# A trunk layer on one core: earlier loads at the MLP's two borders and six residual buffers in a projection's tail

## The chip, the cores and the metric

The kernel runs on one core of a Trainium2 chip. The metric is the device time of one execution in microseconds. Before the change it is 3756.28 us, the median of three runs (3750.0 to 3760.29). Five engines work side by side, each in the order of its own instruction list: TensorE (PE) multiplies, VectorE (DVE), ScalarE (ACT) and GpSimd (POOL) work on tiles, and SyncE (SP) issues most of the DMA transfers. An instruction that waits holds all that stand behind it on its engine; SP's list is a queue of transfers in the same sense.

## The reference, cut to what matters

One layer over 2048 positions of width 1024, in float32:

```
for l in range(DEPTH):                       # DEPTH = 1
    proj = rms_norm(h, norm_mix_w[l]) @ w_in[l]
    y_rwkv = rwkv7_group(proj[..., :RWKV_COLS], ...)       # scan, width 512
    y_diff = diff_attn_group(proj[..., RWKV_COLS:], ...)   # block-causal, width 512
    h = h + concatenate([y_rwkv, y_diff], -1) @ w_out[l]
    h = h + memory_cross_attn(rms_norm(h, norm_mem_w[l]), rms_norm(mem, norm_src_w[l]), ...)
    hn = rms_norm(h, norm_mlp_w[l])
    h = h + square(relu(hn @ w_up[l])) @ w_down[l]         # 1024 -> 4096 -> 1024
return rms_norm(h, norm_final_w)
```

## The kernel before

Activations lie with features on the 128 partitions and 512 positions in a tile; a block is 512 positions, and there are four. Every large product is done in three passes: an operand is split into `hi` (an ACT copy to fp32r) and `lo = raw - hi` (DVE for activations, POOL for weights), and PE adds hi·hi, hi·lo and lo·hi. Weights come in halves of 128 x 4 x 128 (`wraw`, two buffers), and each half gives 12 matmuls of 128x512.

Three stages follow each other.

- **The first phase** runs the input projection as a list of `Item`s through `inproj_stream` (L599), which asks for weights two halves ahead (`li <= i + 2`), and between its pieces the RWKV units and attention. The list ends with 32 items from `wy_items` (L711), eight for each block: `w_out[0:512]` times the RWKV output, added to the residual. For each of them `pre(m)` loads a tile `xres` of the residual from the DRAM buffer `s_xT` (L731), `post(m)` adds the product to it on DVE (L738) and stores it back through ACT's queue (L739). `xres` takes its buffer from the tag `mix`, which has two. The last 24 of these items run in the tail of the phase with little else beside them.
- **The middle stage** (`m_stream` for blocks 0 and 1) isn't touched.
- **The last `m_stream`** takes blocks 2 and 3 together (`NSB == 2`, `s` = 0 and 1). Its MLP has two borders. `mo_forms` (L1296) ends the memory attention and builds for each k of 0 to 3 the seven operand forms that the fast scheme for the up projection needs ("11", "t1", "21", "22", "t3", "t2", "t4"), each split into `bfh` and `bfl`. `up_pairs` (L1341) then makes the hidden tiles two at a time, f = 0, 2, ..., 30 and a drain at 32, seven products of 12 matmuls for each pair, into `ps_a`, `ps_b` and `ps_c`; `emit` (L1363) stores each hidden tile to the DRAM buffer `s_hid`. After it, the down projection loads residual tiles `ht` and hidden tiles in four groups `fg` of eight: `load_hid` (L1533) loads `hraw`, ACT makes `hdh` (L1541), DVE makes `hdl` (L1542), and `down_mm` multiplies them with `w_down` (`load_w`, L161) into `ps_dn` (L186 to L188).

The program is written in one order, and a scheduler, which simulates a timeline while the program is built, sets the order on each engine from it.

Of the kernel before, what the change touches and what calls it, by code (L numbers as in the profile page):

```python
# [8 lines left out]
F32 = mybir.dt.float32  # L9
F32R = mybir.dt.float32r  # L10
# [6 lines left out]
P = 128  # L17
# [20 lines left out]
def f32(ap):  # L38
    return ap.bitcast(F32)
# [539 lines left out]
class Item:  # L579
    def __init__(self, blk, src, post, pre=None, n=TB, nh=2, vt=None):  # L580
        self.blk, self.src, self.post, self.pre, self.n, self.nh, self.vt = blk, src, post, pre, n, nh, vt


def fold_half(g, it, hf, w, st):
# [14 lines left out]
def inproj_stream(g, pool, items, st):  # L599
    nc = g.nc  # L600
    flat = [(it, hf) for it in items for hf in range(it.nh)]
    ready = []
    li = 0
    for i, (it, hf) in enumerate(flat):
        while li < len(flat) and li <= i + 2:
            it2, h2 = flat[li]
            raw = pool.tile([P, 4, P], F32, tag="wraw", name="wraw", bufs=2)
            if it2.vt:
                src = it2.src[h2 * P:(h2 + 1) * P].rearrange("p (k c) -> p k c", c=P)
            else:  # L610
                src = it2.src[h2 * 512:(h2 + 1) * 512].rearrange("(k p) c -> p k c", p=P)
            nc.sync.dma_start(out=raw, in_=src)
            hi = pool.tile([P, 4, P], F32R, tag="whi", name="whi", bufs=3)
            lo = pool.tile([P, 4, P], F32R, tag="wlo", name="wlo", bufs=3)
            nc.scalar.activation(out=hi, in_=raw, func=AF.Copy)  # L615
            nc.gpsimd.tensor_tensor(out=lo, in0=raw, in1=f32(hi), op=ALU.subtract)  # L616
            ready.append((hi, lo))
            li += 1
        if it.vt:
            yield from fold_half(g, it, hf, ready[i], st)  # L620
            continue
        if hf == 0:
            if it.pre:
                it.pre()
            ps = g.ps_acc.tile([P, TB], F32, tag="acc", name="ps_acc")
        hi, lo = ready[i]
        xs = st[it.blk][0]
        o = ps[:, 0:it.n]
        for kk in range(4):
            k = 4 * hf + kk  # L630
            nc.tensor.matmul(o, hi[:, kk, :], xs[k][0], start=(k == 0), stop=False)  # L631
            nc.tensor.matmul(o, hi[:, kk, :], xs[k][1], start=False, stop=False)  # L632
            last = k == 4 * it.nh - 1
            nc.tensor.matmul(o, lo[:, kk, :], xs[k][0], start=False, stop=last)  # L634
            if last:
                it.post(ps)
            yield
# [73 lines left out]
def wy_items(g, pool, st, blk, key):  # L711
    nc = g.nc
    cs = slice(blk * TB, (blk + 1) * TB)
    xts = {}

    def pre(m):
        def f():
            if m == 0:
                ys = []
                for k in range(4):  # L720
                    kk = k + 4 * ((blk + 1) % 2)
                    raw = pool.tile([P, TB], F32, tag="xsl", name="yraw", bufs=3)
                    nc.sync.dma_start(out=raw, in_=g.s.yT[k * P:(k + 1) * P, cs])
                    hi = pool.tile([P, TB], F32R, tag=f"xhi{kk}", name="yhi", bufs=1)
                    lo = pool.tile([P, TB], F32R, tag=f"xlo{kk}", name="ylo", bufs=1)
                    nc.scalar.activation(out=hi, in_=raw, func=AF.Copy)
                    nc.vector.tensor_tensor(out=lo, in0=raw, in1=f32(hi), op=ALU.subtract)
                    ys.append((hi, lo))
                st[key] = [ys]
            xt = pool.tile([P, TB], F32, tag="mix", name="xres", bufs=2)  # L730
            nc.sync.dma_start(out=xt, in_=g.s.xT[m * P:(m + 1) * P, cs])  # L731
            xts[m] = xt
        return f

    def post(m):
        def f(ps):
            xt = xts[m]
            nc.vector.tensor_tensor(out=xt, in0=ps, in1=xt, op=ALU.add)  # L738
            nc.scalar.dma_start(out=g.s.xT[m * P:(m + 1) * P, cs], in_=xt)  # L739
        return f  # L740
    return [Item(key, g.i.w_out[0, :, m * P:(m + 1) * P], post(m), pre(m), TB, 1) for m in range(KD)]


def phase1(g, er):
# [551 lines left out]
def mo_forms(g, mc, wp, fx, O, B, tsl, accs, tag):  # L1296
# [14 lines left out]
    for k in range(4):  # L1311
        bw = {}
        for e in range(2):
            m = k + 4 * e
            wh, wl = load_w(g, wp, g.s.mb[:, m * P:(m + 1) * P])
            for s in range(2):
                xt = mc.px.tile([P, TB], F32, tag="xt", name="xt", bufs=mc.nxt)
                nc.sync.dma_start(out=xt, in_=g.s.hT[m * P:(m + 1) * P, tsl[s]])
                ps = mc.ps_acc.tile([P, TB], F32, tag="acc", name="ps_mo2")
                yield from mm3g(g, ps, wh, wl, lambda k: O[k][s][0], lambda k: O[k][s][1])  # L1320
                nc.vector.tensor_tensor(out=xt, in0=ps, in1=xt, op=ALU.add)
                nc.scalar.dma_start(out=g.s.hT[m * P:(m + 1) * P, tsl[s]], in_=xt)
                b = fx.tile([P, TB], F32, tag="bw", name="bw", bufs=4)
                nc.scalar.activation(out=b, in_=xt, func=AF.Copy, scale=g.col("nmlp", m))
                add_stat(g, mc.px, xt, accs[s], m == 0, "h")
                bw[e, s] = b
                if e == 0 and s == 1:
                    nc.vector.tensor_tensor(out=bw[0, 0], in0=b, in1=bw[0, 0], op=ALU.subtract)
                    split("t1", bw[0, 0])
                else:  # L1330
                    split(("11", "21", "22")[e + s], b)
            yield
        nc.vector.tensor_tensor(out=bw[0, 1], in0=bw[1, 1], in1=bw[0, 1], op=ALU.subtract)
        split("t3", bw[0, 1])
        nc.vector.tensor_tensor(out=bw[0, 0], in0=bw[1, 1], in1=bw[0, 0], op=ALU.subtract)
        split("t2", bw[0, 0])
        nc.vector.tensor_tensor(out=bw[1, 0], in0=bw[1, 0], in1=bw[0, 0], op=ALU.subtract)
        split("t4", bw[1, 0])


def up_pairs(g, mc, wp, B, SB, mlp_scale, tag):  # L1341
# [30 lines left out]
    acc = lambda nm: mc.ps_acc.tile([P, TB], F32, tag="acc", name=nm)  # L1372
    tmp = lambda tg, nb, nm: wp.tile([P, TB], F32, tag=tg, name=nm, bufs=nb)
    prev = None
    for f in range(0, 33, 2):
        if f < 32:
            raw = {}
# [30 lines left out]
        if f < 32:  # L1408
            prod(a, split(raw[0, 1]), "21", False)
            emit(a, f, 0)  # L1410
            c = acc("ps_c")
            prod(c, split(s1), "t1", True)
            s3 = sub(raw[0, 0], raw[1, 0])
            prod(b, split(s3), "t3", False)
            r67 = tmp("wraw", 2, "r67")
            add(r67, b, p1)
            add(r67, c, r67)
            emit(r67, f + 1, 1)
            prev = (f, b, c, p1, r6, raw[1, 1], sub(raw[0, 1], s2))
            yield  # L1420


def m_stream(g, mc, wp, blk0, NSB, Y=None, ahead=None):
# [92 lines left out]
    if NSB == 2:  # L1516
        with ExitStack() as e2:
# [1 line left out]
            accs = [mc.px.tile([P, TB], F32, tag=f"acc{s}", name="acc", bufs=1) for s in range(NSB)]  # L1519
            B = {}  # L1520
            yield from mo_forms(g, mc, wp, fx, O, B, tsl, accs, t1)
            yield from up_pairs(g, mc, wp, B, SB, mlp_scale, t0)
    with ExitStack() as e2:
        ip = e2.enter_context(tc.tile_pool(name="p3b", bufs=2, reuse_waits="tile"))
        ht = [[None] * NSB for _ in range(KD)]
        for m in range(KD):
            for s in range(NSB):
                t = ip.tile([P, TB], F32, tag="ht", name="ht", bufs=mc.nact)
                nc.sync.dma_start(out=t, in_=g.s.hT[m * P:(m + 1) * P, tsl[s]])
                ht[m][s] = t  # L1530
        tg = (t0, t1)

        def load_hid(fg, f, rows):  # L1533
            r0 = (fg * KD + f) * P
            row = []
            for s in range(NSB):
                raw = ip.tile([P, TB], F32, tag="t", name="hraw", bufs=8)
                nc.sync.dma_start(out=raw, in_=g.s.hid[r0:r0 + P, s * TB:(s + 1) * TB])
                hi = act[s].tile([P, TB], F32R, tag=tg[fg % 2] + "h", name="hdh", bufs=KD)
                lo = act[s].tile([P, TB], F32R, tag=tg[fg % 2] + "l", name="hdl", bufs=KD)  # L1540
                nc.scalar.activation(out=hi, in_=raw, func=AF.Copy)  # L1541
                nc.vector.tensor_tensor(out=lo, in0=raw, in1=f32(hi), op=ALU.subtract)  # L1542
                row.append((hi, lo))
            rows.append(row)
        nxt = []
        if NSB == 2:
            for f in range(KD):
                load_hid(0, f, nxt)
        for fg in range(4):
            HID, nxt = nxt, []  # L1550
            for f in range(0 if NSB == 2 else KD):
                c0 = (fg * KD + f) * P
                wh, wl = load_w(g, wp, g.i.w_up[0, :, c0:c0 + P])
# [21 lines left out]
                nc.vector.tensor_tensor(out=ht[m][s], in0=ht[m][s], in1=ps, op=ALU.add)  # L1575
            if fg < 3:
                for m in range(KD):
                    w = down(m)
                    for s in range(NSB):
                        yield from down_mm(m, s, w)  # L1580
                    if NSB == 2:
                        load_hid(fg + 1, m, nxt)
                    yield
        for s in range(NSB):
            acc = mc.px.tile([P, TB], F32, tag=f"acc{s}", name="accf", bufs=1)
# [125 lines left out]
```

## Time and profile before

| what | value |
|---|---|
| median of three runs | 3756.28 us |
| profiled execution: its own time | 3755.66 us |
| its span, first to last instruction | 3753.9 us |
| mean granted TensorE clock | 0.966 |
| tail of the first phase (24 `xres` items) | 1307 to 1416 us |
| `mo_forms` to `up_pairs` | 3044 to 3057 us |
| `up_pairs` to the down projection | 3357 to 3384 us |

The views are read so. A row of waits says engine, waiting tile and line, then what it waited for, with the total in us, how many times, and the longest. A row of windows gives a stretch in us, its length, the busy time and count of PE, PE's weight loads, DVE, ACT and POOL, then the granted clock (1.00 is 2.4 GHz, 0.50 is 1.2 GHz), the busy share of the DMA engines and GB/s. A row of a timeline gives the start in us, the duration, engine, line, operation, output <- inputs and count, and in brackets how long the engine had been idle and what ended that; a row with a count above 1 joins several instructions, and its duration is their sum or stretch. For a DMA the duration is that of the issue, not of the transfer. A row of a tile gives line, engine and operation, count, the shortest, median and longest duration in ns, and the first and last start.

### The profile page before, as it was taken

How to read it: one execution, taken by the hardware profiler on the slowest of the kernel's cores; microseconds unless marked ns; L12 is line 12 of the kernel's file. 1: busy time of each engine (PE TensorE's matmuls, PEld its weight loads, DVE VectorE, ACT ScalarE, POOL GpSimd, SP SyncE). 2: the span in 40 equal slices, each digit the busy share in tenths (PEclk: the TensorE clock that was granted, in tenths of full speed). 3: DMA queues.
4: the chain of work that ended last, by engine and by line, in shares of the span. 5: the costliest groups of instructions: out<-in, count | busy, mean ns of one | idle time of the engine just before them, and what ended most of it. 6: DMA issues, size and time to landing. Idle time of an engine off the chain costs nothing. (4 is left out here: it accounts for less than half of the span.)

```text
span 3753.9 us, 58334 instructions
## 1 busy us (share of the span) xinstructions
PE 3549.6 (95%) x21105; PEld 2837.0 (76%) x21105; DVE 2075.2 (55%) x4201; ACT 1801.4 (48%) x3958; POOL 1538.8 (41%) x1243
## 2 busy tenths in 40 slices
PE   7999999999999878899999989999999999979998
PEld 5767767776767767678787777888878878868887
DVE  4456666675573636465566766666633565634212
ACT  5354464454455526554455765555543443323213
POOL 4524324423424534354535435353353364432235
PEclk9989999999989899999999999999999999989999
DMA  4343343333335674343323424232252243335223
GB/s 151 107 127 88 80 130 87 88 109 88 88 88 155 208 210 142 102 127 93 114 79 118 139 74 145 79 113 78 85 156 90 88 132 107 106 128 168 87 58 107
DMA packets 584503, 424.10 MB, mean 113 GB/s; under 512 B 67235, under 2 KB 493302, under 8 KB 584214
## 3 DMA queue, kind: packets, MB, share of 16 engines
q1 hardware_dynamic: 543350, 346.33, 31.7%
q10 hardware_dynamic: 37280, 67.13, 5.1%
q0 software_dynamic: 3584, 6.92, 0.8%
q8 instruction: 166, 2.72, 0.3%
q14 instruction: 123, 1.01, 0.1%
HBM read 327.92 MB, written 92.34 MB: 112 GB/s over the span
## 5 line engine op out<-in xcount | busy, mean ns | idle before, releaser
L170 POOL TENSOR_TENSOR wlo<-wraw,whi 128x512 fp32r<-128x512 f32 x456 | 609.1, 1337 | 1026.0 <-ACT whi L169 959.7
L616 POOL TENSOR_TENSOR wlo<-wraw,whi 128x512 fp32r<-128x512 f32 x288 | 414.2, 1440 | 591.6 <-ACT whi L615 489.3
L169 ACT ACTIVATE whi<-wraw 128x512 fp32r<-128x512 f32 x456 | 286.1, 628 | 494.5 <-PE ps_dn L187 300.0
L186 PE MATMUL ps_dn<-hdh,whi 128*128 128x512 f32 x1024 | 402.5, 395 | 21.4 <-ACT hdh L1541 19.6
L187 PE MATMUL ps_dn<-hdl,whi 128*128 128x512 f32 x1024 | 402.6, 394 | 0.3 <-DVE hdl L1566 0.3
L188 PE MATMUL ps_dn<-hdh,wlo 128*128 128x512 f32 x1024 | 400.0, 394 | 2.7 <-POOL wlo L170 2.7
L631 PE MATMUL ps_acc<-xhi,whi 128*128 128x512 f32 x832 | 341.4, 411 | 19.5 <-ACT carry L278 18.8
L634 PE MATMUL ps_acc<-xhi,wlo 128*128 128x512 f32 x832 | 342.5, 412 | 2.3 <-POOL wlo L616 2.3
L632 PE MATMUL ps_acc<-xlo,whi 128*128 128x512 f32 x832 | 339.7, 409 | 0.0
L615 ACT ACTIVATE whi<-wraw 128x512 fp32r<-128x512 f32 x288 | 180.4, 628 | 264.2 <-PE ps_acc L632 99.0
L1048 ACT ACTIVATE pt<-ps_s,nmx 128x512 f32<-128x512 f32 (+3 forms) x320 | 197.9, 619 | 143.9 <-DVE nmx L1047 118.8
L1575 DVE TENSOR_TENSOR ht<-ht,ps_dn 128x512 f32<-128x512 f32 x128 | 87.6, 684 | 306.6 <-PE ps_dn L188 306.3
L186 PEld LDWEIGHTS ps_dn<-hdh,whi 128*128 128x128 f32 x1024 | 193.8, 189 | 62.1 <-ACT hdh L1541 20.5
L1047 DVE TENSOR_REDUCE nmx<-ps_s 128x1 f32<-128x512 f32 (+3 forms) x320 | 192.3, 605 | 74.8 <-PE ps_s L1044 70.7
L188 PEld LDWEIGHTS ps_dn<-hdh,wlo 128*128 128x128 f32 x1024 | 193.5, 189 | 44.7 <-POOL wlo L170 5.7
L187 PEld LDWEIGHTS ps_dn<-hdl,whi 128*128 128x128 f32 x1024 | 193.6, 189 | 39.9 <-DVE hdl L1566 0.5
L631 PEld LDWEIGHTS ps_acc<-xhi,whi 128*128 128x128 f32 x832 | 160.4, 193 | 69.1 <-ACT carry L278 24.7
L186 PE MATMUL ps_up<-h2h,whi 128*128 128x512 f32 x512 | 201.2, 394 | 0.9 <-DVE t L1561 0.9
L188 PE MATMUL ps_up<-h2h,wlo 128*128 128x512 f32 x512 | 201.0, 393 | 0.8 <-POOL wlo L170 0.8
L187 PE MATMUL ps_up<-h2l,whi 128*128 128x512 f32 x512 | 201.4, 393 | 0.0
L634 PEld LDWEIGHTS ps_acc<-xhi,wlo 128*128 128x128 f32 x832 | 160.0, 192 | 49.9 <-issue 10.7
L632 PEld LDWEIGHTS ps_acc<-xlo,whi 128*128 128x128 f32 x832 | 160.1, 192 | 39.7 <-issue 7.0
(379 smaller groups left out, 8773.8 us busy)
## 6 DMA issues: line engine op xcount, KB each, us to landing
wraw<-in_w_in_dram SPq DMA_DIRECT2D x208, 256.0 KB
wraw<-in_w_down_dram SPq DMA_DIRECT2D x208, 256.0 KB
wraw<-in_w_up_dram SPq DMA_DIRECT2D x128, 256.0 KB
s_hT<-xt ACTq DMA_DIRECT2D x64, 256.0 KB
wfr<-in_w_up_dram SPq DMA_DIRECT2D x64, 256.0 KB
s_hid<-hid ACTq DMA_DIRECT2D x64, 256.0 KB
hraw<-s_hid SPq DMA_DIRECT2D x64, 256.0 KB
wraw<-in_w_out_dram SPq DMA_DIRECT2D x56, 256.0 KB
```

What stands on the lines that cost most here:

```text
L169: nc.scalar.activation(out=hi, in_=raw, func=AF.Copy)
L170: nc.gpsimd.tensor_tensor(out=lo, in0=raw, in1=f32(hi), op=ALU.subtract)
L186: nc.tensor.matmul(ps, whi(k), ahi(k), start=(k == 0), stop=False)
L187: nc.tensor.matmul(ps, whi(k), alo(k), start=False, stop=False)
L188: nc.tensor.matmul(ps, wlo(k), ahi(k), start=False, stop=(k == nk - 1))
L615: nc.scalar.activation(out=hi, in_=raw, func=AF.Copy)
L616: nc.gpsimd.tensor_tensor(out=lo, in0=raw, in1=f32(hi), op=ALU.subtract)
L631: nc.tensor.matmul(o, hi[:, kk, :], xs[k][0], start=(k == 0), stop=False)
L632: nc.tensor.matmul(o, hi[:, kk, :], xs[k][1], start=False, stop=False)
L634: nc.tensor.matmul(o, lo[:, kk, :], xs[k][0], start=False, stop=last)
L1047: nc.vector.tensor_reduce(out=nmx[:, m, c:c + 1], in_=ps[:, 0:w], axis=AX.X, op=ALU.max, negate=True)
L1048: nc.scalar.activation(out=pt[:, cw(c)], in_=ps[:, 0:w], func=AF.Exp, bias=nmx[:, m, c:c + 1], accum_out=sm[:, m, c:c + 1])
```

## The change

It has four parts. `xres` gets a tag of its own with six buffers, and its load moves out of `pre` into `load(m)`, which `inproj_stream` calls right after the item's weight transfer. In `mo_forms`, after each k, form t2 is built first, then t3 and t4, and the split of "22" goes last. `load_hid` becomes a function of its own that loads straight into the `lo` tile (`hdl`), from which ACT makes `hdh` and DVE subtracts in place, so that `hraw` and its eight buffers go; `up_pairs` itself loads the first group of hidden tiles, those of s = 0 inside the last pair (f = 30) and those of s = 1 after the drain. In the down projection the 16 `ht` loads go from ahead of everything to the place where each is first used in group 0, and group 0 begins with the weights of m = 0 and 1 together, both products of s = 0, then both of s = 1.

```
 inproj_stream:
             nc.sync.dma_start(out=raw, in_=src)
+            if it2.load:
+                it2.load()
 wy_items:
-            xt = pool.tile([P, TB], F32, tag="mix", name="xres", bufs=2)
+        return f
+
+    def load(m):
+        def f():
+            xt = pool.tile([P, TB], F32, tag="xres", name="xres", bufs=6)
             nc.sync.dma_start(out=xt, in_=g.s.xT[m * P:(m + 1) * P, cs])
             xts[m] = xt
 mo_forms:
-                else:
-                    split(("11", "21", "22")[e + s], b)
+                elif e + s < 2:
+                    split(("11", "21")[e], b)
             yield
+        nc.vector.tensor_tensor(out=bw[0, 0], in0=bw[1, 1], in1=bw[0, 0], op=ALU.subtract)
+        split("t2", bw[0, 0])
         nc.vector.tensor_tensor(out=bw[0, 1], in0=bw[1, 1], in1=bw[0, 1], op=ALU.subtract)
         split("t3", bw[0, 1])
-        nc.vector.tensor_tensor(out=bw[0, 0], in0=bw[1, 1], in1=bw[0, 0], op=ALU.subtract)
-        split("t2", bw[0, 0])
         nc.vector.tensor_tensor(out=bw[1, 0], in0=bw[1, 0], in1=bw[0, 0], op=ALU.subtract)
         split("t4", bw[1, 0])
+        split("22", bw[1, 1])
+def load_hid(g, mc, tag, f, s):
+    lo = mc.act[s].tile([P, TB], F32R, tag=tag + "l", name="hdl", bufs=KD)
+    hi = mc.act[s].tile([P, TB], F32R, tag=tag + "h", name="hdh", bufs=KD)
+    g.nc.sync.dma_start(out=f32(lo), in_=g.s.hid[f * P:(f + 1) * P, s * TB:(s + 1) * TB])
+    g.nc.scalar.activation(out=hi, in_=f32(lo), func=AF.Copy)
+    g.nc.vector.tensor_tensor(out=lo, in0=f32(lo), in1=f32(hi), op=ALU.subtract)
+    return hi, lo
 up_pairs:
+        if f == 30:
+            first.append([load_hid(g, mc, tag, i, 0) for i in range(KD)])
+    first.append([load_hid(g, mc, tag, i, 1) for i in range(KD)])
+    return first
 m_stream, down projection:
             if fg < 3:
                 for m in range(KD):
-                    w = down(m)
-                    for s in range(NSB):
-                        yield from down_mm(m, s, w)
+                    if NSB == 2 and fg == 0 and m != 1:
+                        for i in range(m, max(2, m + 1)):
+                            load_h(i)
+                    if NSB == 2 and fg == 0 and m < 2:
+                        ws = [down(0), down(1)] if m == 0 else ws
+                        for i in range(2):
+                            yield from down_mm(i, m, ws[i])
+                    else:
+                        w = down(m)
+                        for s in range(NSB):
+                            yield from down_mm(m, s, w)
                     if NSB == 2:
-                        load_hid(fg + 1, m, nxt)
+                        nxt.append([load_hid(g, mc, (t0, t1)[(fg + 1) % 2], (fg + 1) * KD + m, s) for s in range(2)])
```

SP's list at the border from `up_pairs` to the down projection, before: four `w_down` halves (`wraw`), 16 `ht`, eight `hraw`, then the next half. These rows are the last two `ht` and the rows up to that half.

```order
L1529 DMA ht_34026<-s_hT_61 128x512
L1529 DMA ht_34028<-s_hT_61 128x512
L1538 DMA hraw_34030<-s_hid_62 128x512
L1538 DMA hraw_34036<-s_hid_62 128x512
L1538 DMA hraw_34042<-s_hid_62 128x512
L1538 DMA hraw_34048<-s_hid_62 128x512
L1538 DMA hraw_34054<-s_hid_62 128x512
L1538 DMA hraw_34060<-s_hid_62 128x512
L1538 DMA hraw_34066<-s_hid_62 128x512
L1538 DMA hraw_34072<-s_hid_62 128x512
L166 DMA wraw_34278<-in_w_down_dram 128x4x128
```

The same place now. The first row stands behind 25 other loads of hidden tiles, which follow the last weights of the up projection; they belong to groups 0 and 1.

```order
L1355 DMA hdl_34059<-s_hid_62 128x512
L166 DMA wraw_34086<-in_w_down_dram 128x4x128
L1355 DMA hdl_34614<-s_hid_62 128x512
L1355 DMA hdl_34619<-s_hid_62 128x512
L166 DMA wraw_34092<-in_w_down_dram 128x4x128
L1355 DMA hdl_34064<-s_hid_62 128x512
L1355 DMA hdl_34692<-s_hid_62 128x512
L1355 DMA hdl_34697<-s_hid_62 128x512
L166 DMA wraw_34098<-in_w_down_dram 128x4x128
L1355 DMA hdl_34069<-s_hid_62 128x512
L1555 DMA ht_34078<-s_hT_61 128x512
```

What moved: the hidden tiles of two groups stand ahead of the first `w_down` half, and `ht` behind them all.

DVE's list at the end of `mo_forms` for one k, before: 31145 is the tile of t3, 31107 of t2, 31196 of t4 and 31234 of "22".

```order
L1333 TENSOR_TENSOR bw_31145<-bw_31234,bw_31145 128x512
L1335 TENSOR_TENSOR bw_31107<-bw_31234,bw_31107 128x512
L1309 TENSOR_TENSOR bfl_31240<-bw_31234,bfh_31239 128x512
L1337 TENSOR_TENSOR bw_31196<-bw_31196,bw_31107 128x512
L1309 TENSOR_TENSOR bfl_31245<-bw_31145,bfh_31244 128x512
L1309 TENSOR_TENSOR bfl_31250<-bw_31107,bfh_31249 128x512
L1309 TENSOR_TENSOR bfl_31255<-bw_31196,bfh_31254 128x512
```

And now:

```order
L1343 TENSOR_TENSOR bw_31107<-bw_31234,bw_31107 128x512
L1345 TENSOR_TENSOR bw_31145<-bw_31234,bw_31145 128x512
L1347 TENSOR_TENSOR bw_31196<-bw_31196,bw_31107 128x512
L1319 TENSOR_TENSOR bfl_31241<-bw_31107,bfh_31240 128x512
L1319 TENSOR_TENSOR bfl_31246<-bw_31145,bfh_31245 128x512
L1319 TENSOR_TENSOR bfl_31251<-bw_31196,bfh_31250 128x512
L1319 TENSOR_TENSOR bfl_31255<-bw_31234,bfh_31254 128x512
```

The t2 subtraction and its `bfl` come one and two places earlier, and the `bfl` of "22" is last.

SP's list near the start of the program, where the transposed input is stored to `s_xT` (`xsl`) and the first weights are loaded, before:

```order
L250 DMA s_xT_57<-xsl_274 128x512
L250 DMA s_xT_57<-xsl_288 128x512
L250 DMA s_xT_57<-xsl_302 128x512
L612 DMA wraw_233<-in_w_in_dram 128x4x128
L250 DMA s_xT_57<-xsl_316 128x512
L612 DMA wraw_371<-in_w_in_dram 128x4x128
L250 DMA s_xT_57<-xsl_330 128x512
```

And now:

```order
L250 DMA s_xT_57<-xsl_274 128x512
L738 DMA xres_11748<-s_xT_57 128x512
L738 DMA xres_11977<-s_xT_57 128x512
L250 DMA s_xT_57<-xsl_288 128x512
L738 DMA xres_12178<-s_xT_57 128x512
L250 DMA s_xT_57<-xsl_302 128x512
L250 DMA s_xT_57<-xsl_316 128x512
L613 DMA wraw_233<-in_w_in_dram 128x4x128
L613 DMA wraw_371<-in_w_in_dram 128x4x128
L738 DMA xres_12408<-s_xT_57 128x512
L250 DMA s_xT_57<-xsl_330 128x512
```

The first six residual loads, whose buffers nothing has used yet, have moved to the start of the program, each behind the store that it reads; the first `xres` load of the program before stood some 400 places later.

## Rows read from the trace of the kernel before

**Rows 1.** The page: busy time, share and count of each engine.
```profile
PE 3549.6 (95%) x21105; PEld 2837.0 (76%) x21105; DVE 2075.2 (55%) x4201; ACT 1801.4 (48%) x3958; POOL 1538.8 (41%) x1243
```

**Rows 2.** Waits of PE over the whole span: xres and the two borders.
```profile
PE ps_acc L631 <- DVE xres L738: 21.9, 12, 5.1
PE ps_dn L186 <- ACT hdh L1541: 19.6, 1, 19.6
...
PE ps_b L1360 <- ACT bfh L1308: 4.9, 1, 4.9
```

**Rows 3.** Timeline around the border from the up to the down projection.
```profile
3351.60 0.50 PE L1360 MATMUL ps_b<-bfh,wfh 128*128 128x512 f32 x1 [0.78 <-DVE r L1370]
...
3353.03 5.67 SPq L166 DMA_DIRECT2D wraw<-in_w_down_dram  x3
...
3356.32 0.63 ACT L169 ACTIVATE whi<-wraw 128x512 fp32r<-128x512 f32 x1 [2.66 <-DMA wraw<-in_w_down_dram]
...
3358.75 10.69 SPq L1529 DMA_DIRECT2D ht<-s_hT  x16
...
3369.75 6.31 SPq L1538 DMA_DIRECT2D hraw<-s_hid  x8
3376.40 5.25 ACT L1541 ACTIVATE hdh<-hraw 128x512 fp32r<-128x512 f32 x8 [16.77 <-DMA hraw<-s_hid]
...
3377.08 2.38 PE L186 MATMUL ps_dn<-hdh,whi 128*128 128x512 f32 x4 [19.63 <-ACT hdh L1541]
3377.12 5.25 DVE L1542 TENSOR_TENSOR hdl<-hraw,hdh 128x512 fp32r<-128x512 f32 x8 [18.15 <-ACT hdh L1541]
```

**Rows 4.** Windows: in mo_forms' border, the first down matmuls, the end of up_pairs.
```profile
3046.00:3048.00 2.00, 0.00 (x0) 0.00 (x0) 2.00 (x2) 0.63 (x1) 2.00 (x3) 0.50 0.41 122
...
3376.00:3380.00 4.00, 2.92 (x6) 2.10 (x7) 2.86 (x5) 3.35 (x6) 0.00 (x0) 0.50 1.06 389
3380.00:3384.00 4.00, 4.00 (x12) 3.08 (x12) 3.27 (x6) 3.06 (x6) 0.00 (x0) 0.57 1.03 356
...
3307.00:3357.00 50.00, 49.22 (x213) 39.57 (x212) 17.02 (x24) 15.11 (x26) 15.96 (x12) 1.00 0.21 72
```

**Rows 5.** Timeline around the border from mo_forms to up_pairs.
```profile
3046.81 1.75 DVE L1335 TENSOR_TENSOR bw<-bw 128x512 f32<-128x512 f32 x1
...
3049.27 0.80 PE L1360 MATMUL ps_b<-bfh,wfh 128*128 128x512 f32 x1 [4.92 <-ACT bfh L1308]
...
3056.76 0.65 PE L158 MATMUL psb<-ident,rstdg 128*128 128x128 f32 x4 [0.94 <-POOL rstdg L153]
```

**Rows 6.** Windows: the tail of the first phase.
```profile
1307.00:1416.00 109.00, 83.17 (x358) 65.34 (x357) 35.91 (x81) 27.68 (x59) 37.29 (x31) 0.93 0.71 207
```

**Rows 7.** Waits of PE, DVE and the SP queue in 1307 to 1416 us.
```profile
PE ps_acc L631 <- DVE xres L738: 20.8, 11, 5.1
PE ps_s L1043 <- DVE xres L738: 5.0, 1, 5.0
...
DVE xres L738 <- DMA xres<-s_xT: 62.4, 19, 7.9
...
SPq L731 <- DMA s_xT<-xres: 54.1, 19, 6.8
```

**Rows 8.** The tile xres in 1307 to 1416 us: its additions.
```profile
L738 DVE TENSOR_TENSOR xres<-ps_acc,xres x24: 683/692/693, 1316.3 to 1414.6; 128x512 f32<-128x512 f32 x24
```

**Rows 9.** Timeline in the tail: one turn of a weight buffer.
```profile
1354.43 0.40 SPq L612 DMA_DIRECT2D wraw<-in_w_out_dram  x1
...
1358.85 0.63 ACT L615 ACTIVATE whi<-wraw 128x512 fp32r<-128x512 f32 x1 [4.27 <-DVE xres L738]
...
1359.56 1.29 POOL L616 TENSOR_TENSOR wlo<-wraw,whi 128x512 fp32r<-128x512 f32 x1 [3.62 <-ACT whi L615]
...
1361.41 0.40 SPq L612 DMA_DIRECT2D wraw<-in_w_out_dram  x1
```

**Rows 10.** Timeline at the start of the program.
```profile
24.30 0.60 ACT L249 ACTIVATE xsl<-ps_xt 128x512 f32<-128x512 f32 x1 [0.47 <-DMA s_xT<-xsl]
```

More of the change, by code (lines that the diff above doesn't have):

```diff
@@ L581, in __init__ @@
         self.blk, self.src, self.post, self.pre, self.n, self.nh, self.vt = blk, src, post, pre, n, nh, vt
+        self.load = None
 def fold_half(g, it, hf, w, st):
@@ L740, in post @@
         return f
-    return [Item(key, g.i.w_out[0, :, m * P:(m + 1) * P], post(m), pre(m), TB, 1) for m in range(KD)]
+    out = [Item(key, g.i.w_out[0, :, m * P:(m + 1) * P], post(m), pre(m), TB, 1) for m in range(KD)]
+    for m, it in enumerate(out):
+        it.load = load(m)
+    return out
 def phase1(g, er):
@@ L1374, in up_pairs @@
     prev = None
+    first = []
     for f in range(0, 33, 2):
@@ L1521, in m_stream @@
             yield from mo_forms(g, mc, wp, fx, O, B, tsl, accs, t1)
-            yield from up_pairs(g, mc, wp, B, SB, mlp_scale, t0)
+            first = yield from up_pairs(g, mc, wp, B, SB, mlp_scale, t0)
     with ExitStack() as e2:
@@ L1525, in m_stream, with load_h @@
         ht = [[None] * NSB for _ in range(KD)]
-        for m in range(KD):
+        def load_h(m):
             for s in range(NSB):
@@ L1530, in m_stream @@
                 ht[m][s] = t
[L1531 to L1535, printed above, removed]
-            for s in range(NSB):
[L1537 to L1545, printed above, removed]
+        if NSB == 1:
+            for m in range(KD):
+                load_h(m)
         if NSB == 2:
-            for f in range(KD):
-                load_hid(0, f, nxt)
+            nxt = [list(r) for r in zip(*first)]
         for fg in range(4):
-            HID, nxt = nxt, []
+            HID, nxt = (nxt, []) if NSB == 2 else ([], [])
             for f in range(0 if NSB == 2 else KD):
@@ L1577, in m_stream @@
                 for m in range(KD):
-                    w = down(m)
-                    for s in range(NSB):
-                        yield from down_mm(m, s, w)
+                    if NSB == 2 and fg == 0 and m != 1:
[9 more added lines that the diff above has]
+                            yield from down_mm(m, s, w)
                     if NSB == 2:
-                        load_hid(fg + 1, m, nxt)
+                        nxt.append([load_hid(g, mc, (t0, t1)[(fg + 1) % 2], (fg + 1) * KD + m, s) for s in range(2)])
                     yield
```

## The prediction

> **What bounds the kernel now.** I read the page's busy times first: PE is busy 95% of the span and the next engine, PE's weight loads apart, 55% [rows 1]. So time can only come from where PE stands still or runs at the low clock. The waits of PE over the span name three such places that the change touches: 21.9 us for `xres` in the first phase, 19.6 us in one piece before the first down matmul, which waits for ACT's `hdh`, and 4.9 us at the entry of `up_pairs` [rows 2]. The timeline shows what stands behind the 19.6. The weights are early: SP begins to ask for `w_down` at 3353.03, and ACT copies the first half at 3356.32. But then SP issues 16 `ht` (10.69 us) and only at 3369.75 the `hraw` loads, whose first lands 6.65 us later, at 3376.40 [rows 3]. Nothing needs `ht` that early: a product is added to it only when it is done. The wait for `xres` lies nearly all in the tail of the first phase. In its 109 us PE is busy 83.17, idle 25.8, at a mean clock of 0.93 [rows 6]. In the waits 25.8 us of PE (20.8 and 5.0) stand against DVE's `xres`, DVE's `xres` stands 62.4 us against its DMA, and SP holds that load for 54.1 us until an earlier store of `xres` has landed [rows 7]. So the chain there is a ring: load, add, store, and the same buffer's next load. Its additions run from 1316.3 to 1414.6, 24 of them, 4.27 us apart in the mean [rows 8]; with two buffers one turn is twice that, 8.5 us.
>
> **The border from the up to the down projection.** Gone: the 19.63 us [rows 3], and the low clock after it. In 3377.08 to 3384.00, 6.9 us, 18 matmuls start [rows 4], where the step in the last 50 us of `up_pairs` is 49.22 / 213 = 0.231 us [rows 4], 4.2 us for 18. I put 2.5 us on it, since the last may reach over the edge. Together 22.1 us.
>
> Added: nothing in instructions (32 hidden tiles of groups 0 and 1 still need a load, an ACT copy and a DVE subtraction), but their place moves into the last 50 us or so of `up_pairs`, and 26 of the loads now stand ahead of the first `w_down` half on SP. Each waits until its buffer, a weight or form tile of the last pairs, is done with. The one just ahead of the first half takes a tile of the t3 product, which in the last pair has the products t4 and 22 behind it: 24 matmuls, 5.5 us before the end. The weights are thus asked for about 5.2 us before PE runs dry. A `w_down` half took at most 3.29 us from the request to ACT's copy, and a load in the burst 6.65 [rows 3]. With the first: landed at -1.9, the ACT copy (0.63) by about -0.9 since it queues behind a few `hdh`, the gap 0 to 1.5 us, as the third pass waits for POOL's `wlo`, 1.3 us more. With the second: landed at +1.5, PE dry for 2 to 3 us. I take 1 us, nearer the first row, since the DMA engines are at 0.21 there before [rows 4] and the hidden tiles come paced by their buffers.
>
> The cover for the moved work: DVE is busy 17.02 and ACT 15.11 of those 50 us [rows 4]. An `hdl` costs 5.25 / 8 = 0.66 us [rows 3], 32 of them 21 us, so DVE goes to about 38 of 50, and some are left for after the border. The new wait is on DVE: behind three `hdl` in its list stands the sum `r` of the last pair, for which PE already waited 0.78 us at 3351.60 [rows 3]. I expect this to become 1 to 2 us, so it costs 0.5. Net for this border: 22.1 - 1 - 0.5 = 20.6, ends 22 (all hidden) and 17 (PE dry for 3 us, `r` 2 us late).
>
> DVE's t2 subtraction took 1.75 us [rows 5] in a stretch in which POOL was busy without a break [rows 4], while `hdl`, with POOL idle [rows 4], took 0.66. The Trainium skill, "SBUF — State Buffer", section "Who interferes with whom", says that a DVE instruction with two SBUF inputs and a GpSimd instruction that reads SBUF shut each other out, since they share a port pair. The trace agrees, 1.75 against 0.66. If `hdl` tiles meet POOL's 12 instructions of the last 50 us [rows 4], each meeting costs DVE some 1.1 us, 13 us in all, and DVE would stand at 51 of 50 us: `r` and the tiles behind it would be some 4 us late. By the rule the border would gain 16 to 17 and the kernel take 3717; by the rows without it, 3713. I stay with the second, since the loads are paced by PE's products and need not meet POOL each time.
>
> **The border into `up_pairs`.** PE waits 4.92 us until ACT's `bfh` of t2 [rows 5]. That subtraction moves one place up, ahead of one of 1.75 us, so PE resumes some 1.7 us earlier. But it resumes into three or four matmuls and soon needs the `bfl` tiles and later the row scale `psb` (at 3056.76, 0.94 us of wait for POOL [rows 5]), which stands behind the same DVE work as before. What is won at the wait is lost there. I put 0, ends -1 (a loss) and 2.
>
> **The tail of the first phase.** With six buffers a turn of 8.5 us and even 12 us gives at most 2 us for an item, so the ring stops binding. Next are three bounds. PE: 83.17 us x 0.93 / 24 = 3.2 us an item at full clock [rows 6]. DMA: weights, load and store are 3 x 262 KB; the stretch moved 207 GB/s at a share of 0.71 [rows 6], so 292 GB/s full, 2.7 us. Weights: two `wraw` buffers, one turn from issue to issue 1361.41 - 1354.43 = 6.98 us [rows 9], or 3.5 an item; in it ACT's copy waited for DVE's `xres`, because the store's issue stands ahead of it on ACT, and without that it is shorter, say 3.3 to 3.8 with fuller DMA engines. I take 3.5. The most that can be won is the idle 25.8 and the clock's 83.17 x 0.07 = 5.8, 31.6 us. Of it the weights keep 24 x (3.5 - 3.2) = 7 and the entry and exit of the stretch (the 5.0 us wait [rows 7] is at its end) about 3: 22 us, ends 8 (3.9 us an item and a clock that stays low) and 31.
>
> **The rest.** Six `xres` loads come to the start of the program, each behind the landing of a store to `s_xT`. ACT's `xsl` already waits for such a landing at 24.30, 0.47 us [rows 10], so it costs a wait of SP of under a microsecond at each; weights stand behind it, but PE has work. I put 0.5 lost, ends 0 and 2. PE's waits for `xres` outside the tail are 21.9 - 20.8 = 1.1 us [rows 2, 7]: gain 1. Elsewhere the scheduler shuffles neighbours in phase one; I give that 0, ends -5 and 5.
>
> Sum: 20.6 + 22 + 0 - 0.5 + 1 = 43 us. The profiled execution took 3755.66, its median of three runs 3756.28, so 0.6 more; from there 3756.3 - 43 = 3713.
>
> **The rivals.**
> - *The weights bind the tail.* Fuller DMA engines stretch the landing until a turn of `wraw` is 7.8 us, 3.9 an item. For it: two buffers only, and a turn of 6.98 already. Against it: ACT's copy no longer waits for the store. Gain in the tail 8 instead of 22: 3727.
> - *The hidden tiles hold back the weights at the border.* 26 loads ahead of `w_down`, landings as in the burst (6.65 us), copies behind `hdh` on ACT: PE dry for about 6 us, and the low clock again for 2.5, with later halves late by about 1.5. The gain is 12: 3722. For it: SP's order. Against it: DMA at 0.21 there.
> - *The change doesn't do what it says.* `xres` isn't with the weights but where the scheduler puts it, as the six at the start show, so the ring of the tail only shifts (gain 4 or less), and the border gives 5 or less because the loads wait for buffers of the last pair: about 3748. Against it: from item 8 on, loads and weights alternate on SP.
> - *The tail becomes slower than before.* If loads, weights and stores come bunched, a weight lands late; `xres` once stood 7.9 us for its transfer [rows 7]. A `wraw` turn is landing plus 0.63 and 1.29 and a request, 2.3 us; the tail breaks even at a turn of 8.5, a landing of 6.2, and loses the border's 20.6 too at 24 x (period - 4.27) = 20.6, a period of 5.1, a landing of 8. At 9 us of landing: 5.65 an item, 33 lost, 12 net: 3768. One `xres` came near that; the mean did not.
>
> **How the numbers follow.** The forecast, both places gained: 0.65, its own range 3700 to 3724. Weights bind the tail 0.15, border held back 0.10, not as said 0.05, slower tail 0.05. A measurement of this kernel can tell some 0.3%, 11 us, from no change. The first three cases are all faster than that: 0.90; not as said is 0.05 for within it; slower 0.05. Both gains at their ends, 22 and 31, give 3702, with the shuffle's 5 us 3698; the two middle rivals reach 3727, together with a bad shuffle 3733. I take 3699 to 3733.
>
> **What would show it.** Right: no wait of PE over 3 us before the first down matmul and a granted clock of 1.00 through it, `hdl` and `hdh` inside the last pairs of `up_pairs`, PE's waits for `xres` in the tail under 5 us, and additions about 3.5 us apart. If they are 3.9 and PE waits for `whi` or `wlo` at L615 and L616, the weights bind. If the first down matmul waits for `whi`, the border is held back. If `r` or `hid` of the last pair waits long on DVE, the moved subtractions weren't covered. The prediction is wrong if either gain is under half of its term.

## The result, and the profile after

The changed kernel takes 3719.53 us (median of four runs, 3718.53 to 3731.22) against 3757.12 of the kernel before on the same chip (3750.0 to 3760.29, four runs): a ratio of 0.9905, with a 95% interval of 0.9882 to 0.9929. It is 37.6 us faster; 43 were forecast, and 3719.53 lies in the forecast's own range of 3700 to 3724. Its profiled execution took 3718.53 us with a span of 3716.8 and a mean granted clock of 0.975. The experiments ran on three chips, on which the kernel before took 3753.97 to 3761.78 us, so kernels of different chips are compared by their ratios to it. Two executions, the profiled one of e2 (3934.15 us) and one of e3 (4182.72 us), were disturbed, with granted clocks of 0.834 and 0.772, and are left out of the medians and the table.

The span can be cut at four instructions that both kernels have, read from the first and last starts in the tile rows of PE's matmuls: the last `ps_fold` before the tail, the first `ps_wo` of the middle stage, the first `ps_b` of `up_pairs` and the last `ps_dn`. The table has all profiled executions that are used below, in us.

| kernel | start to last ps_fold | to first ps_wo (tail) | to first ps_b (middle) | to last ps_dn (borders) |
|---|---|---|---|---|
| before | 1302.6 | 116.9 | 1616.6 | 703.0 |
| changed | 1301.8 | 96.1 | 1619.8 | 684.3 |
| e1: xres alone | 1306.7 | 96.4 | 1619.5 | 704.0 |
| e3: mo_forms alone | 1299.3 | 115.8 | 1616.1 | 703.9 |
| e4: six buffers, load in pre | 1292.7 | 96.7 | 1625.3 | 703.7 |
| e5: changed, three buffers | 1300.3 | 104.5 | 1621.8 | 682.9 |
| e6: changed, group 1 on GpSimd | 1309.7 | 98.0 | 1623.3 | 685.4 |
| e7: changed, three weight buffers | 1260.7 | 115.1 | 1621.7 | 684.8 |
| e8: e6 and e7 | 1262.5 | 115.8 | 1620.6 | 690.7 |
| e9: before, three weight buffers | 1264.0 | 122.4 | 1606.2 | 701.0 |
| e10: changed, group 1 held back | 1312.0 | 98.3 | 1611.4 | 678.1 |
| e11: e7 and e10 | 1261.2 | 114.8 | 1616.4 | 680.4 |

For the profiled pair: 0.8 us won up to the last `ps_fold`, 20.8 in the tail, 3.2 lost in the middle, 18.7 won from `up_pairs` on, 37.1 in all. The first and third columns vary by about 10 us on either side between executions whose code there hardly differs; the second and fourth mostly agree within 2 or 3 us (e6 and e8, with the same code at the borders, differ by 5.3), and the verdicts below go by them. Attention work can cross the first cut: the second column holds 378 or 379 matmuls with six buffers, 387 or 388 with two, 404 in e5, and 455 to 460 with three weight buffers. Where the counts differ, the first two columns have to be taken together.

**The border to the down projection.** The timeline of the changed kernel, where [rows 3] had the 19.63 us:

```profile
3320.73 14.58 SPq L1355 DMA_DIRECT2D hdl<-s_hid  x14
...
3331.85 2.02 DVE L1357 TENSOR_TENSOR hdl<-hdl,hdh 128x512 fp32r<-128x512 f32 x3 [0.62 <-ACT hdh L1356]
...
3332.18 0.39 PE L1380 MATMUL ps_b<-bfh,wfl 128*128 128x512 f32 x1
3333.81 1.15 ACT L1356 ACTIVATE hdh<-hdl 128x512 fp32r<-128x512 f32 x2 [0.66 <-DMA hdl<-s_hid]
3334.47 0.69 DVE L1357 TENSOR_TENSOR hdl<-hdl,hdh 128x512 fp32r<-128x512 f32 x1 [0.60 <-ACT hdh L1356]
3335.08 0.68 DVE L1390 TENSOR_TENSOR r<-ps_b,p 128x512 f32<-128x512 f32 x1
3335.40 0.38 SPq L166 DMA_DIRECT2D wraw<-in_w_down_dram  x1
...
3335.82 0.80 PE L1380 MATMUL ps_b<-bfh,wfh 128*128 128x512 f32 x1 [3.25 <-DVE r L1390]
...
3341.04 0.61 ACT L169 ACTIVATE whi<-wraw 128x512 fp32r<-128x512 f32 x1
...
3341.53 0.52 PE L1380 MATMUL ps_c<-bfl,wfh 128*128 128x512 f32 x1
...
3343.98 0.40 PE L1380 MATMUL ps_c<-bfh,wfl 128*128 128x512 f32 x1
3344.22 0.39 PE L186 MATMUL ps_dn<-hdh,whi 128*128 128x512 f32 x1
```

PE goes from the last `ps_c` matmul to the first `ps_dn` without a pause, though the first `w_down` half was asked for only at 3335.40 and copied 5.6 us later. But 12 us earlier PE stands 3.25 us for the sum `r`, which took 0.78 before. When the last `ps_b` matmul ahead of the stand ends, at 3332.57, DVE is in a bunch of three `hdl`. They take it until 3333.87, then it stands 0.60 us for the `hdh` of a fourth, whose load had just landed, and that `hdl` takes the place until `r` starts at 3335.08. So `r` comes 2.5 us late, 1.9 of it behind work of DVE and 0.6 behind a load. The windows over the same place (columns as in [rows 4]) show what the stand costs after it:

```profile
3332.00:3336.00 4.00, 0.75 (x4) 0.32 (x3) 3.37 (x6) 2.17 (x4) 0.00 (x0) 0.87 0.82 265
3336.00:3340.00 4.00, 4.00 (x10) 3.13 (x11) 2.54 (x5) 1.91 (x4) 0.00 (x0) 0.50 0.91 308
3340.00:3344.00 4.00, 4.00 (x16) 3.18 (x15) 3.57 (x5) 2.85 (x5) 1.30 (x1) 0.77 0.91 282
...
3284.00:3334.00 50.00, 48.57 (x210) 39.05 (x208) 31.11 (x43) 26.50 (x46) 17.60 (x13) 1.00 0.51 172
```

The clock falls to 0.50 and is back near 3341.5: 14 matmuls start from 3335.82 on in some 6.1 us, where the step of 0.231 would make 3.2 of it. The last row answers to the 50 us of [rows 4]: DVE went from 17.0 to 31.1 us busy and the DMA share from 0.21 to 0.51.

**The entry of `up_pairs`.** PE's wait for `bfh`, 4.92 us in [rows 5], and its wait for the row scale:

```profile
3028.21 0.80 PE L1380 MATMUL ps_b<-bfh,wfh 128*128 128x512 f32 x1 [3.50 <-ACT bfh L1318]
...
3033.81 0.50 PE L1380 MATMUL ps_b<-bfl,wfh 128*128 128x512 f32 x1 [1.43 <-DVE bfl L1319]
...
3038.49 0.65 PE L158 MATMUL psb<-ident,rstdg 128*128 128x128 f32 x4 [1.16 <-POOL rstdg L153]
```

The stand is 1.4 us shorter, then PE waits 1.43 for `bfl`. From the first `ps_b` to the matmul that waits for `psb` it is 3056.76 - 3036.1 = 20.7 before and 3038.49 - 3017.7 = 20.8 now.

**The tail.** Window, waits of PE, DVE, SP and ACT, and the tile `xres`, all between its first and last addition; they answer to [rows 6 to 8]:

```profile
1308.60:1394.00 85.40, 75.04 (x348) 59.23 (x346) 34.61 (x79) 26.68 (x57) 35.93 (x30) 1.00 0.81 238
```

```profile
PE ps_acc L637 <- POOL wlo L619: 3.0, 4, 1.3
...
PE ps_acc L634 <- ACT whi L618: 1.9, 1, 1.9
...
DVE xres L745 <- PE ps_acc L637: 21.5, 11, 3.8
...
SPq L738 <- DMA s_xT<-xres: 23.3, 14, 4.7
SPq L613 <- POOL wlo L619: 16.1, 13, 2.1
...
ACT whi L618 <- DMA wraw<-in_w_out_dram: 30.5, 11, 6.6
```

```profile
L745 DVE TENSOR_TENSOR xres<-ps_acc,xres x24: 678/691/692, 1308.6 to 1394.0; 128x512 f32<-128x512 f32 x24
```

DVE's addition now waits for PE's product and no longer for its load. The 24 additions lie 85.4 / 23 = 3.71 us apart instead of 4.27, the clock is 1.00, and PE's waits for `xres`, 25.8 us in [rows 7], come to 0.8 in the whole program. The weights are a wait now: ACT's copy stands 30.5 us for their landing, and SP may ask for the next only when GpSimd has finished with the last. But little of it reaches PE, which is busy 75.04 of the 85.4 us (3.1 us an item, with the attention work beside the items), and waits 4.9 us for `wlo` and `whi`.

### The profile page after: what moved, and what is told of

Same layout as the page of the kernel before. It is cut to its first block, busy times and chain, and to the rows that moved or that the text cites. A ratio compares the mean times of both kernels' runs of the same rounds, so it can differ in the third digit from the quotient of the medians.

```text
span 3716.8 us, 58302 instructions
## 1 busy us (share of the span) xinstructions
PE 3529.4 (95%) x21105; PEld 2820.6 (76%) x21105; DVE 2081.7 (56%) x4201; ACT 1799.0 (48%) x3958; POOL 1539.4 (41%) x1243
## 5 line engine op out<-in xcount | busy, mean ns | idle before, releaser
L634 PE MATMUL ps_acc<-xhi,whi 128*128 128x512 f32 x832 | 342.6, 412 | 21.9 <-ACT carry L278 20.9
```

## The experiments

**e1 and e4: is it the buffers or the place of the request?** e1 is the kernel before with the whole `xres` part; e4 has the tag and the six buffers alone, and the load stays in `pre`:

```
-            xt = pool.tile([P, TB], F32, tag="mix", name="xres", bufs=2)
+            xt = pool.tile([P, TB], F32, tag="xres", name="xres", bufs=6)
```

> The kernel before with the xres part alone (own tag, six buffers, loads with the weights). Theory: the two large gains are separate; this one gives what the first phase of the changed kernel gained, 22 us by the first down matmul of the middle stage (1672.0 to 1649.5), less the 4 us that the middle stage lost if that loss comes from the xres part: 3735 to 3739. Rival: the tail's gain needs the rest of the change or is given back later; then 3745 or more. Rival: the loss of 4 us in the middle stage belongs to the rewritten down projection; then the whole 22 stay, 3734 to 3736.

> The kernel before with six buffers and a tag of their own for xres, but the load still asked for in pre, when the item's product begins. Theory: the buffers open the ring, and the scheduler asks for a load as soon as its buffer is free wherever the program has it, so this gives the tail's whole gain, 3734 to 3739. Rival: the place of the request matters; with the load at the item's start its 2.5 us and more of transfer stand before the addition, the gain is 5 to 12, 3744 to 3751.

e1 took 3741.81 us (ratio 0.9951, 0.9932 to 0.997), e4 3737.3 (0.9934, 0.9909 to 0.9958). e4 is in the range of its theory; e1 is 3 us above its own and below the rival's 3745. Their tails are 96.4 and 96.7 us, their additions 85.7 and 84.3 us from first to last:

```profile
L745 DVE TENSOR_TENSOR xres<-ps_acc,xres x24: 678/692/692, 1313.0 to 1398.7; 128x512 f32<-128x512 f32 x24
```

```profile
L738 DVE TENSOR_TENSOR xres<-ps_acc,xres x24: 677/692/694, 1301.1 to 1385.4; 128x512 f32<-128x512 f32 x24
```

Theory held for both in the tail. SP's list is the same in the two programs, transfer for transfer, and so are those of ACT, DVE and GpSimd: here the scheduler asked for the loads at the same places, wherever the program has them. So the new place of the request did nothing; the buffers did it all.

**e2 and e3: the two borders apart.** e2 is the kernel before with the new `load_hid`, the `ht` loads and the order of the first down products; e3 has the order in `mo_forms` alone.

```
 e2, in up_pairs:
+        if f == 30:
+            first.append([load_hid(g, mc, tag, i, 0) for i in range(KD)])
+    first.append([load_hid(g, mc, tag, i, 1) for i in range(KD)])
 e3, in mo_forms:
+        nc.vector.tensor_tensor(out=bw[0, 0], in0=bw[1, 1], in1=bw[0, 0], op=ALU.subtract)
+        split("t2", bw[0, 0])
...
+        split("22", bw[1, 1])
```

> The kernel before with load_hid, the ht loads and the order of the first down products alone. Theory: 18.9 us, the wait of 19.6 and the low clock after it gone, less a new wait of 3.3 us for DVE's sum r and low clock after that: 3737 to 3739, and the same wait for r of about 3 us in the trace. Rival: the wait for r comes from the other parts of the change; then r waits under 1 us and the time is 3732 to 3734. If the middle stage loses 4 us here too, the loss belongs to this part.

> The kernel before with the new order in mo_forms alone. Theory: what PE wins at its wait for bfh (4.9 to 3.5 us) it loses in the next 10 us to the tiles that are ready no earlier; 0, 3754 to 3759. Rival: the won time stays, 1.5 to 3 us with the clock that rises earlier: 3753 to 3755.

e2 took 3737.24 us (0.9934, 0.9913 to 0.9955), as its theory had it. Its profile isn't in the table; PE waits 3.3 us for `r` in it, which is not counted, so that this part alone brings the wait isn't shown. By their ratios e1 and e2 gain 18 and 25 us, each within 8 or so, which fits two separate gains but is too coarse to show that they add. e3 took 3756.09 (0.9991, 0.997 to 1.0012), no difference; its last column is 703.9 against 703.0, though PE's wait for `bfh` is 3.5 us in it as in the changed kernel. What was won at that wait is lost behind it.

**e5: three buffers instead of six.**

```
-            xt = pool.tile([P, TB], F32, tag="xres", name="xres", bufs=6)
+            xt = pool.tile([P, TB], F32, tag="xres", name="xres", bufs=3)
```

> The changed kernel with three buffers for xres instead of six. Theory: what binds the ring is the number of buffers: one turn is load, add, store of 8.5 us, so three give 2.8 us an item, less than the 3.7 us at which the changed kernel's tail runs; the whole gain stays, the same time as the changed kernel within 8 us, about 3720 to 3728. Rival: with a request three items ahead and fuller DMA engines the turn grows to 12 us or more, 4 us an item; 7 to 12 us of the tail's gain are lost, 3727 to 3735.

3719.81 us (0.9894, 0.9874 to 0.9914), within noise of the changed kernel. The tail is 104.5 us, 8 of the 20.8 given back, and DVE again waits for the load:

```profile
PE ps_acc L634 <- DVE xres L745: 1.1, 4, 0.4
...
PE ps_s L1053 <- DVE xres L745: 0.8, 1, 0.8
...
DVE xres L745 <- DMA xres<-s_xT: 14.1, 8, 2.8
```

The 8 us are not the ring's. The tail of the changed kernel and that of e5 (columns as in [rows 4]):

```profile
1301.80:1397.90 96.10, 82.54 (x378) 64.72 (x376) 38.30 (x88) 32.44 (x70) 38.44 (x32) 0.99 0.80 234
1300.30:1404.80 104.50, 90.31 (x404) 69.81 (x402) 48.50 (x118) 36.98 (x83) 40.68 (x33) 0.95 0.79 233
```

PE is idle 13.6 us in the one and 14.2 in the other, and waits only 1.1 and 0.8 us for `xres`; e5 has 26 matmuls more here, which the changed kernel had done before the cut. Theory holds, and the rival's loss of 7 to 12 us isn't there: three buffers are enough for this tail.

**e6: group 1's subtractions on GpSimd.**

```
-    g.nc.vector.tensor_tensor(out=lo, in0=f32(lo), in1=f32(hi), op=ALU.subtract)
+    (eng or g.nc.vector).tensor_tensor(out=lo, in0=f32(lo), in1=f32(hi), op=ALU.subtract)
...
+                        nxt.append([load_hid(g, mc, (t0, t1)[(fg + 1) % 2], (fg + 1) * KD + m, s, nc.gpsimd if fg == 0 else None) for s in range(2)])
```

> The changed kernel with the subtractions of the hidden tiles of group 1 (the 16 that are not needed for another 40 us) on GpSimd instead of DVE. Theory: the 3.3 us that PE waits for r in the last pair, and the low clock after it, come from DVE, which has these subtractions in its list ahead of r, each waiting for its load; with them gone r waits under 1.5 us, and the time falls by 3 to 6 us. Rival: r is late because the loads themselves are late (the load queue and the copies on ACT), and group 0's tiles hold DVE as well; then r still waits 2 to 3 us and the time is the same within 2 us. Rival: GpSimd becomes late with the weights' wlo at the first down products, and PE waits for wlo there; 0 to 5 us slower.

3731.94 us (0.9919, 0.9894 to 0.9944), by its ratio not to be told from the changed kernel, and 685.4 in the last column against 684.3. PE's waits in 3330 to 3400 us of its trace:

```profile
PE ps_dn L188 <- POOL wlo L170: 2.5, 2, 1.6
PE ps_b L1380 <- DVE r L1390: 1.9, 1, 1.9
PE ps_dn L186 <- ACT whi L169: 1.4, 1, 1.4
```

Theory failed: `r` still waits 1.9 us. That is hardly less than the 2.2 us of e5, which has the border of the changed kernel unchanged:

```profile
3339.97 2.71 DVE L1357 TENSOR_TENSOR hdl<-hdl,hdh 128x512 fp32r<-128x512 f32 x4 [0.62 <-ACT hdh L1356]
...
3343.33 0.50 PE L1380 MATMUL ps_b<-bfh,wfh 128*128 128x512 f32 x1 [2.24 <-DVE r L1390]
```

In e6 a single `hdl` stands ahead of `r`, and DVE stood 2.88 us for its copy:

```profile
3346.06 0.84 DVE L1357 TENSOR_TENSOR hdl<-hdl,hdh 128x512 fp32r<-128x512 f32 x1 [2.88 <-ACT hdh L1356]
```

So with group 1's subtractions gone, late loads and copies hold `r` instead, as the first rival has it, with 1.9 us just under its 2 to 3. The second rival is right as well: GpSimd's `wlo` and ACT's `whi` are now late for the first down products. From the row scale `psb` to the first of these it took 303.4 us instead of 305.7, and from there to the last 361.5 instead of 357.7.

**e10: group 1 held back whole.** Groups 1 to 3 go through eight raw buffers of the down projection's pool again, which isn't there before `up_pairs` ends; group 0 stays as in the change.

```
+    raw = pool.tile([P, TB], F32, tag="t", name="hraw", bufs=8) if pool else f32(lo)
+    g.nc.sync.dma_start(out=raw, in_=g.s.hid[f * P:(f + 1) * P, s * TB:(s + 1) * TB])
```

> The changed kernel with the hidden tiles of groups 1 to 3 loaded through eight raw buffers of the down projection's own pool, as before the change, so that no tile of group 1 can come ahead of the end of up_pairs on SP, ACT or DVE; group 0 as in the changed kernel. Theory: group 1's tiles are what makes r late (in the queue of loads, in the copies and in the subtractions); PE's wait for r falls from 3.3 to under 1 us with the clock at 1.00, and from the first ps_b of up_pairs to the last down matmul it takes 678 to 680 us instead of 683.6. Rival: group 0's own tiles hold r; then it still waits over 2 us, and the stretch is within 1.5 us of 683.6. Rival: group 1's tiles come too late for their products; PE waits for hdh at the second group, and the stretch is longer.

3713.98 us (0.9888, 0.9866 to 0.9911), the last column 678.1, 6.2 us under the changed kernel's. PE's wait for `r`, the windows at the border and the first down matmul:

```profile
PE ps_b L1381 <- DVE r L1391: 0.8, 1, 0.8
```

```profile
3334.00:3338.00 4.00, 3.21 (x15) 2.30 (x14) 1.52 (x3) 1.07 (x2) 0.00 (x0) 1.00 0.45 150
3338.00:3342.00 4.00, 4.00 (x19) 3.24 (x18) 3.63 (x6) 1.79 (x3) 0.72 (x1) 1.00 0.60 175
3342.00:3346.00 4.00, 4.00 (x19) 3.28 (x18) 2.46 (x4) 1.79 (x3) 1.86 (x2) 1.00 0.81 239
```

```profile
3343.10 0.39 PE L186 MATMUL ps_dn<-hdh,whi 128*128 128x512 f32 x1
```

The wait is back at 0.8, the clock stays at 1.00 through the border, and no wait took their place. e11, with the same border, has 0.78; the profiles with group 1 ahead have 1.9 to 3.3. So group 1's tiles were the cause: their loads, copies and subtractions together, since moving the subtractions alone (e6) didn't do it. The gain is read in the last column; by the ratios, 0.9888 against 0.9905, the two kernels can't be told apart.

**e7, e8, e9 and e11: a third raw weight buffer in the first phase.** One number in `inproj_stream`, on the changed kernel (e7), with e6 (e8), on the kernel before (e9), and with e10 (e11):

```
-            raw = pool.tile([P, 4, P], F32, tag="wraw", name="wraw", bufs=2)
+            raw = pool.tile([P, 4, P], F32, tag="wraw", name="wraw", bufs=3)
```

> The changed kernel with three instead of two buffers for the raw weights of the first phase's item list. Theory: the tail now runs at 3.7 us an item because the weights bind it (SP waits 16 us for GpSimd's wlo before it may ask for weights); with a third buffer it comes to 3.3 to 3.5, 4 to 10 us faster, and additions lie that close. Rival: DMA binds (share 0.81 there, 24 items of three transfers each); then a third buffer only asks earlier and lands later, the same within 4 us.

> Both: group 1's subtractions on GpSimd and three raw weight buffers in the first phase. Theory: the two act in different stages, so their effects add: 7 to 16 us below the changed kernel. Rival: both nothing; the same within 4 us.

> The kernel before, with nothing but a third buffer for the raw weights of the first phase's item list. Theory: the third weight buffer saves its time ahead of the tail (PE's waits for carry and wlo between 0 and 1260 us), where xres doesn't bind; so it is worth the same 20 us without the change: 3736 to 3744. Rival: it only pays once the ring of xres is open; then under 6 us, 3750 to 3758.

> Group 1 held back and three raw weight buffers in the first phase: the two act in different stages, so about 4 us below the kernel with the three weight buffers alone (3698.6), 3692 to 3697. Rival: the held-back tiles bring nothing; 3697 to 3700.

e7 took 3698.64 us (0.9833, 0.9812 to 0.9854), e8 3700.69 (0.9843, 0.9822 to 0.9865), e9 3714.46 (0.9898, 0.9879 to 0.9918), e11 3688.48 (0.9832, 0.9813 to 0.9852, against a median of 3753.97 on its chip). The first three gained more than forecast. e11 does so in its time alone: by the ratios it is level with e7, 0.9832 against 0.9833, because the kernel before was 6 us faster on its chip too. What holding group 1 back is worth beside the third weight buffer shows only in the last column, 680.4 against 684.8. e8's last column is 690.7 where e6, with the same border, had 685.4; in e8 PE also stood 3.1 us for `whi` behind the border, and 1.4 in e6.

For e7 the place wasn't as its theory had it. Its additions:

```profile
L745 DVE TENSOR_TENSOR xres<-ps_acc,xres x24: 666/683/692, 1275.2 to 1367.1; 128x512 f32<-128x512 f32 x24
```

They lie 4.0 us apart, wider than without, because attention work has moved in beside the items: 393 matmuls between e7's first and last addition instead of 348. So whether the weights bound the tail isn't settled by it. The first column falls to between 1260.7 and 1264.0, from 1292.7 to 1312.0 without, but 60 to 70 of its matmuls have gone to the tail. The first two columns together for the kernel before and e9:

```profile
0.00:1419.50 1419.50, 1314.62 (x10378) 984.39 (x10378) 821.03 (x2067) 691.28 (x1662) 552.33 (x502) 0.95 0.42 120
0.00:1386.40 1386.40, 1300.90 (x10390) 967.60 (x10390) 844.10 (x2080) 692.40 (x1669) 550.44 (x501) 0.96 0.43 122
```

That is 33.1 us less with twelve matmuls more: PE stands 19.4 us less and is busy 13.7 us less, at a clock of 0.96 instead of 0.95 (in e3, with the code of the kernel before there, the stretch took 1415.1 us and PE was busy 1308.1, so some of both is scatter). Three of PE's waits fall by 20.7 us; in the kernel before they were 21.9, 18.8 and 9.8:

```profile
PE ps_acc L631 <- DVE xres L738: 16.2, 11, 3.3
...
PE ps_acc L631 <- ACT carry L278: 10.0, 8, 5.0
...
PE ps_acc L634 <- POOL wlo L616: 3.6, 4, 1.1
```

So e9's theory had the place right and half of the size, and its rival, that the buffer only pays once the ring of `xres` is open, is out. Why `carry` comes sooner with a third weight buffer is open. From the changed kernel to e7 the two columns together fall by 1397.9 - 1375.8 = 22.1 us, and from e9 to e7, where only the ring of `xres` and the borders differ, by 10.6.

## Why the prediction was right, and where its sizes were off

- **The border to the down projection**, forecast 20.6: 18.7. The 19.63 us are gone, as said. The gap of 1 us at the first down matmul didn't come. The mis-sized term is the new wait for `r`: put at 0.5 us, it cost 3.25 - 0.78 = 2.5 of wait and 6.1 - 3.2 = 2.9 of low clock, 5.4. The prediction had three `hdl` ahead of `r`; they came in a bunch with a fourth behind it, 1.9 us of DVE's work and 0.6 of standing for a load. And it gave a wait of a few us no price in clock. e10 shows whose tiles these were; with them held back nothing of the addition is left. The stretch behind the border paid for part of it: from the first to the last `ps_dn` it took 3739.07 - 3377.08 = 362.0 us before and 3701.95 - 3344.22 = 357.7 now, 4.3 less, where 2.5 were counted.
- **The signs.** By what the prediction named, the border was not as said on two counts: PE did wait over 3 us (3.25) before the first down matmul, and the clock was not 1.00 through it but fell to 0.50. The sign that it gave for moved subtractions that aren't covered, a long wait for `r`, is the one that came. The gain held because the wait that went was six times as long. In the tail the signs came true or nearly so, with 0.8 us of PE's waits for `xres` and additions 3.71 us apart.
- **DVE and GpSimd.** The 32 `hdl` took 0.76 us in the mean where 0.66 was taken, with single ones of 1.62 beside a GpSimd subtraction (at 3341.95). In e6, with GpSimd at work on tiles of its own, DVE's sixteen took 0.95 and GpSimd's 1.51. The rule of the Trainium skill, "SBUF — State Buffer", section "Who interferes with whom", agrees with these meetings, but they were few: 24 us for 32 tiles is far from the price that 12 of them would have set, and DVE stood at 31 of 50 us. The prediction's alternative by that rule, `r` late by some us, came true from another cause: GpSimd's last work ahead of the stand ended at 3320.70.
- **The entry of `up_pairs`**, forecast 0: 20.7 and 20.8 us, and e3 no difference. Right, by the steps given.
- **The tail**, forecast 22: 20.8 for the pair, 17.5 to 20.8 for the kernels with six buffers and two weight buffers against the two with two. Some 2 us of it are the nine or ten matmuls that the kernels with six buffers had done before the cut (an estimate, at 83.17 / 358 = 0.23 us each [rows 6]). The ring stopped binding, at 3.71 us an item where 3.5 was taken. That the weights came next, as the prediction has it, is only in part borne out: PE's own work, attention included, is 3.1 us an item, and its waits for `wlo` and `whi` are 4.9 us over all 24. The rival that had the weights bind at 3.9 was nearly as close in the period, but not in the sum, since the clock rose to 1.00 and the entry of the tail shortened too.
- **The rest.** The six loads at the start cost 0.1 us (first item matmul at 24.44 instead of 24.34). The last difference, 3.2 us lost in the middle, is where other kernels with the same code vary from 1606 to 1625; it isn't settled, nor needed. It also means that the sum, 6 us off, was closer than the terms deserve by some luck: in this pair the first and third columns moved by 0.8 and 3.2 us, where other executions differ by 10.
- **The rival that the change doesn't do what it says** had its sign right: the loads are not where the program puts them. It was wrong that the ring would stay.

## What to carry to other kernels

When loads move ahead of the work that feeds them, look in each queue and engine list for who stands behind them: an instruction that needs a load in flight holds its engine until the load is there, and those behind it then come in a bunch, as the `hdl` ahead of `r` did. Where a scheduler sets the order, a buffer that comes free is an invitation to run ahead, and the pool or tag from which a tile comes is the way to hold it back. A ring with two buffers is worth a look even where PE's waits hardly name it: one more raw weight buffer, which this change didn't touch, was by itself worth as much as the whole change (0.9898 against 0.9905).

## What the runs showed that was not expected

A stand of PE of 3.25 us was followed by a granted clock of 0.50 for some 6 us; the stand of 0.78 us at the same place, before and in e10, left it at 1.00. Shorter stands were followed by the low clock too: after the 1.89 us of e6 and the 2.24 of e5 matmuls of 0.63 us ran for some 3 us each, between others of 0.40. And two executions whose first 1300 us differ by a few neighbouring instructions came 19 us apart there (1292.7 in e4, 1312.0 in e10), while the stretch from `up_pairs` on repeats within 3 us (701.0 to 704.0 in five executions without the change at the down projection).
